# Two of seven output products moved into the last chunk slots of each scan, and two weight sums made by DMAs

## The chip, the cores and the metric

The kernel runs on one core of one Trainium2 chip. The metric is the device time of one execution in microseconds (us), taken as the median of several runs. TensorE (PE) does the matmuls, VectorE (DVE) and ScalarE (ACT) the elementwise work, GpSimd (POOL) some elementwise work and the issue of some DMAs, and SyncE (SP) issues the other DMAs.

## The reference

The program is a trunk of two layers over 1024 tokens of width 1024, all in float32. Cut to what matters here:

```
x = x + gated_deltanet(rmsnorm(x, norm_w[0]))      # layer 0: chunked delta rule, 16 heads of 128
x = x + mamba2(rmsnorm(x, norm_w[1]))              # layer 1: chunked state-space scan, 32 heads of 64
return rmsnorm(x, final_norm_w)
# the last line of both mixers is the one that the change is about
return o.reshape(b, t, 2048) @ w_out               # (1024 x 2048) @ (2048 x 1024)
```

## The kernel before

Each layer has three stages: input projections with causal convolutions, a scan over eight groups of heads (g = 0 to 7) with eight chunks each, and the output product `y @ w_out`. The work of a scan group is cut into eight slots; in each slot the program advances a few generators by one step: the scan itself (S), the preparation of the next group (I, J) and, in layer 1, `steps1`. A scheduler then sets the final order of the instructions of each engine, except where `keep_in_program_order` holds a DMA in place.

**The output product.** Its 2048 x 1024 weight is seen as a 2 x 2 block matrix, the tokens as two halves, and the product is done by a scheme with seven block products instead of eight. Each needs one weight form of `wf` (x00, s1, s2, x01, s3, s4, x11: a block or a sum of blocks) and one y form (`y_form`: a block of the scan's output or a sum of blocks). A block product has eight K tiles j and four token blocks p. Each of the 32 pairs takes three matmuls of 128 x 512 (`mac`, L411 to L413), because both operands are split into a high and a low part (`split`, L86 by ACT and L87 by DVE). So a product is 96 matmuls, 12 for each j, into four banks of PSUM: either `U` (names ps_proj, ps_pt) or `V` (ps_tr, ps_sc).

**Where the operands come from.** The scan writes its y rows to DRAM (`y0d`, L867 and L868 in layer 0; `y1d`, L1101 and L1103 in layer 1), and `load_y` (L359) reads them back in tiles of 128 x 512 through SP's queue. `load_x` (L383) does so for the weights. The sums of weight blocks differ by layer. In layer 1 they are ready in DRAM: `steps1` has made all four during the scan with 44 DMAs from POOL's queue, of which 16 copy (L338) and 28 accumulate (L340). In layer 0 nothing is made ahead: `w_form` loads the blocks of a sum and POOL adds them (L389). Products 1 and 2 keep the sum s1, s2 in SBUF (`W1`), product 4 (s3) loads two blocks for each j and adds them, product 5 (s4) adds x01 to W1. The y forms of products 1 and 2 go through `N1` (L371) and `Tt` (L374).

**Order of the products.** Product 0 (`early`) runs inside the last four slots of group 7, spread between the last chunk steps of the scan. Its result stays in its four PSUM banks. Then the memory pool of the scan is closed and another opened (`nrm`, tiles woh, wol, yh, yl, Tt, xrow, u). `rest` runs products 1 to 6: product 1 on the V banks, whose split tiles still lie in the old pool (name wy), while the new pool comes up. At product 1's j = 2 the residual rows start to be fetched (`fetch`, L445, twelve DMAs then and four later), ACT copies product 0's banks to `u` (L475), and DVE adds the banks to xrow (L454). Each later product is added to or subtracted from xrow directly (L454, L456) or through `u` (L460 on POOL, L463 on DVE); then comes the RMSNorm of finished rows.

**Names in the rows below.** L803, L811, L820, L838 and L840 are the matmuls of a chunk step of layer 0's scan, whose state S is carried from step to step; L66 transposes a finished head (yn); L867 gates it into the tile yg, and L868 stores that. In layer 1 L1072 to L1076 are the scan's last matmuls.

Of the kernel before, what the change touches and what calls it, by code (L numbers as in the profile page):

```python
# [8 lines left out]
F32 = mybir.dt.float32  # L9
F32R = mybir.dt.float32r  # L10
AF = mybir.ActivationFunctionType
ALU = mybir.AluOpType
# [4 lines left out]
P = 128  # L17
# [7 lines left out]
def hybrid_trunk(  # L25
# [6 lines left out]
    nc = tc.nc  # L32
    x, out = x[0], out[0]
# [284 lines left out]
                                fill=-1e30, base=0, channel_multiplier=-1)  # L318
        return t

    def weight_sums(w_out, nm):

        X = lambda c, k: w_out[k * 1024:(k + 1) * 1024, c * 512:(c + 1) * 512]
        parts = {"s1": ((1, 0), (1, 1)), "s2": ((1, 0), (1, 1), (0, 0)), "s3": ((0, 0), (1, 0)),
                 "s4": ((0, 1), (1, 0), (1, 1), (0, 0))}
        forms = {f"x{c}{k}": X(c, k) for c in range(2) for k in range(2)}
        for f in parts:
            forms[f] = tc.dram_tile([1024, 512], F32, name=f"wo_{nm}{f}")

        def steps():  # L330
            for q in range(4):
                r = slice(q * 256, (q + 1) * 256)
                for i in range(4):
                    for f, p in parts.items():
                        if i < len(p):
                            src, dst = X(*p[i])[r, :], forms[f][r, :]
                            if i == 0:
                                d = nc.gpsimd.dma_start(dst, src)  # L338
                            else:
                                d = nc.gpsimd.dma_start(dst, src, accum_op=ALU.add)  # L340
                            tc.keep_in_program_order(d)
                            yield

        return forms, steps()

    def out_proj(yd, X, made, resid):
# [8 lines left out]
        N1, W1 = [], []  # L355
# [6 lines left out]
        def y_form(i, j, Tt):  # L362
            if i in (0, 3, 5):
                return load_y(*{0: (0, 0), 3: (1, 0), 5: (1, 1)}[i], j)
            if i == 4:
                a, b = load_y(1, 1, j), load_y(0, 1, j, "raw")
                (nc.gpsimd if made else nc.vector).tensor_tensor(out=a, in0=a, in1=b, op=ALU.subtract)
                return a
            if i == 1:
                a, b, d = load_y(0, 0, j), load_y(0, 1, j, "raw"), N1[j // 4][:, j % 4, :]  # L370
                (nc.gpsimd if made else nc.vector).tensor_tensor(out=d, in0=a, in1=b, op=ALU.subtract)  # L371
            else:
                a, d = load_y(*{2: (1, 1), 6: (1, 0)}[i], j), Tt[:, j, :]
# [6 lines left out]
        def load_x(f, j):  # L380
            raw = wring.tile([P, 512], F32, tag=("wr", "wh", "wl")[ring_at[0] % 3], name="wr", bufs=3)
            ring_at[0] += 1
            nc.sync.dma_start(raw, X[f][j * P:(j + 1) * P, :])  # L383
            return raw

        def w_form(f, j):
            if made or f[0] == "x":
                return load_x(f, j)
            add = lambda d, a, b: nc.gpsimd.tensor_tensor(out=d, in0=a, in1=b, op=ALU.add)  # L389
            if f == "s3":  # L390
                a, b = load_x("x00", j), load_x("x10", j)
                add(a, a, b)
                return a
            d = W1[j // 4][:, j % 4, :]
            if f == "s1":
                add(d, load_x("x10", j), load_x("x11", j))
            else:
                add(d, d, load_x({"s2": "x00", "s4": "x01"}[f], j))
            return d

        def pieces(i, j, ring, Tt):
# [25 lines left out]

        banks0 = []

        def early():  # L430
            banks0.extend(U())
            yield from product(0, banks0, in_a(("a0", "a1", "a2", "a3")))

        def rest(npool, nw, on_rows, before_last=lambda: None):
            rows = {t: [npool.tile([P, D], F32, tag="xr", name="xrow", bufs=NT) for _ in range(4)] for t in range(2)}
            Tt = npool.tile([P, 8, 512], F32, tag="T", name="Tt", bufs=1)
            u = npool.tile([P, 4, 512], F32, tag="u", name="u", bufs=1)
            N1.extend(apool.tile([P, 4, 512], F32, tag="a0", name="N1", bufs=2) for _ in range(2))
            if not made:
                W1.extend(apool.tile([P, 4, 512], F32, tag="a1", name="W1", bufs=2) for _ in range(2))  # L440
            half = lambda t, p, c: rows[t][p][:, c * 512:(c + 1) * 512]

            def fetch(t, c):
# [11 lines left out]
                else:  # L455
                    nc.vector.tensor_tensor(out=v, in0=v, in1=pt, op=ALU.subtract)  # L456

            def put_u(t, p, c, op):
                v = half(t, p, c)
                nc.gpsimd.tensor_tensor(out=v, in0=v, in1=u[:, p, :], op=op)  # L460

            def grow(p, pt):
                nc.vector.tensor_tensor(out=u[:, p, :], in0=pt, in1=u[:, p, :], op=ALU.add)  # L463
# [6 lines left out]
            def first(t, p, c):  # L470
                sums[t, p] = rms_first(npool.tile([P, 512], F32, tag="sq", name="sq", bufs=1), rows[t][p], c)

            def d0():
                for p in range(4):
                    nc.scalar.copy(u[:, p, :], banks0[p])  # L475
                    put(0, p, 0, banks0[p], ALU.add)

            def d1(p, pt):
                put(1, p, 0, pt, ALU.add)
                put(1, p, 1, pt, ALU.subtract)  # L480

            def d2(p, pt):
                grow(p, pt)
# [13 lines left out]
                put(1, p, 0, pt, ALU.add)  # L497
                finish(1, p, 0)

            for i, done in ((1, d1), (2, d2), (3, d3), (4, d4), (5, d5)):  # L500
                banks = V() if i % 2 else U()
                for j, _ in enumerate(product(i, banks, in_a(("a2", "a3")) if i == 1 else ring, Tt)):
                    if (i, j) == (1, 2):
                        fetch(0, 0)
                        d0()
                    if (i, j) == (1, 4):
                        fetch(1, 0)
                        fetch(1, 1)
                    if (i, j) == (3, 3):
                        fetch(0, 1)  # L510
                if i == 5:
                    before_last()
                for p in range(4):
                    done(p, banks[p])
# [57 lines left out]
        return yd[g // 4, n // 4][(g % 4) * 256:(g % 4 + 1) * 256, (n % 4) * P:(n % 4 + 1) * P]  # L572

    yd0, yd1 = y_dram("y0d"), y_dram("y1d")
    wo1, steps1 = weight_sums(sw_out, "s")
    wo0 = {f"x{c}{k}": gw_out[k * 1024:(k + 1) * 1024, c * 512:(c + 1) * 512] for c in range(2) for k in range(2)}
    early0, rest0 = out_proj(yd0, wo0, False, lambda n: x[n * P:(n + 1) * P, :])
    early1, rest1 = out_proj(yd1, wo1, True, lambda n: x1d[n])

    with tc.tile_pool(name="gw", bufs=2) as gw:  # L580
# [360 lines left out]
        for g in range(8):  # L941
            J = todo["K"] if g == 0 else js_of(g)
            I = inverse(g + 1) if g < 7 else iter(())
            S = scan(g)
            for slot in range(8):
                if g == 7 and slot > 3:
                    next(early0)
                    if slot < 6:
                        next(early0)
                for c in "SIJ":  # L950
                    if c == "S":
                        next(S, None)
                    elif c == "I":
                        next(I, None)
                    else:
                        next(J, None)
            for _ in I:
                pass
            flush()
            next(S, None)  # L960
            if g < 6:
                for _ in k_products(g + 2):
                    pass
            elif g == 7:
                next(early0)
            next(S, None)
            if g < 7:
                z_weights(g + 1)
# [14 lines left out]
    with tc.tile_pool(name="bpool", bufs=2) as bpool, tc.tile_pool(name="sw", bufs=2) as sw:  # L983
# [145 lines left out]
        for g in range(-1, 8):  # L1129
            its = [bc_halves(g + 1) if g >= 0 else bc0, x_halves(g + 1)] if g < 7 else []  # L1130
            J = (y_ for it in its for y_ in it)
            S = scan(g) if g >= 0 else iter(())
            for slot in range(8):
                if g >= 0:
                    next(steps1, None)
                if g == 7 and slot > 3:
                    next(early1)
                    if slot < 6:
                        next(early1)
                next(S, None)  # L1140
                next(J, None)
            flush()
            if g == 7:
                next(early1)
            next(S, None)
            for _ in early1 if g == 7 else ():
                pass
            if g < 7:
                GS[g + 1]["zw"] = load_zw(bpool, sw_in, (g + 1) * 256, ("a2", "a3"), 2)
# [34 lines left out]
```

## Time and profile before

| what | us |
|---|---|
| median of 3 runs (range) | 2002.54 (1997.89 to 2002.66) |
| the profiled execution, its own time | 1990.88 |
| its span | 1989.1 |
| PE busy in the span | 1886.8 (95%) |
| DVE, ACT, POOL busy | 1427.4, 1078.9, 572.7 |
| scan groups of layer 0, PE busy share in 200 to 800 | 96.6% |
| scan groups of layer 1, PE busy share in 1200 to 1800 | 99.0% |

The profiled execution is 11.7 us (0.6%) shorter than the median of the runs, and outside its span lie 1.8 us. The rows in the section on the trace come from that execution, with times from the start of its span. Matmuls overlap in the pipeline, so a busy PE isn't always a PE at its full rate; the granted clock (PEclk) beside it says how fast TensorE was allowed to run, where 1.00 is 2.4 GHz.

### The profile page before, as it was taken

Reading aid. Unit: us, or ns where it says so; the run is one execution under the profiler, and the core shown is the slowest. Engines: PE = TensorE matmul, PEld = TensorE weight load, DVE = VectorE, ACT = ScalarE, POOL = GpSimd, SP = SyncE. Lnnn points to the kernel's source line nnn. Section 1 sums busy time; section 2 is a strip of 40 time slices with the busy share of each in tenths; the row PEclk is TensorE's granted clock in tenths of the full one; section 3 lists DMA queues with packets and bytes.
Section 4 is the critical chain, followed back from the end, with each engine's and each line's share of the span. In section 5 each row is a group of like instructions: output and inputs, shape, how many; then the busy total and the mean of one; then the engine's idle time right before and its main releaser. Section 6 shows DMA issues by size and latency. Waiting matters only on the chain.

```text
span 1989.1 us, 36021 instructions
## 1 busy us (share of the span) xinstructions
PE 1886.8 (95%) x12782; PEld 1611.4 (81%) x12782; DVE 1427.4 (72%) x3027; ACT 1078.9 (54%) x2933; POOL 572.7 (29%) x934
## 2 busy tenths in 40 slices
PE   7997999999999999998989999999999999999997
PEld 5776888888888888886777788888888888888786
DVE  5787786777668786847689777666576666757677
ACT  5635656565655756554435465454545555554453
POOL 1102111212122212104164033434343342434053
PEclk9997999999999999999999999999999999999999
DMA  4421322233142424237475245455464543246664
GB/s 141 117 54 46 88 67 76 75 71 83 43 104 49 104 49 106 71 106 243 149 262 170 75 146 120 117 130 119 115 135 116 117 99 82 80 127 195 228 225 148
DMA packets 252470, 231.10 MB, mean 116 GB/s; under 512 B 66897, under 2 KB 182274, under 8 KB 252290
## 3 DMA queue, kind: packets, MB, share of 16 engines
q1 hardware_dynamic: 242370, 205.73, 35.5%
q0 software_dynamic: 9920, 23.07, 6.2%
q8 instruction: 100, 1.64, 0.3%
q14 instruction: 80, 0.66, 0.1%
HBM read 199.19 MB, written 52.63 MB: 127 GB/s over the span
## 4 chain that ended last, share of the span: by engine, by line
PE 34%; DMA 6%; DVE 6%; POOL 2%; issue 2%; ACT 2%; SPq 0%; POOLq 0%; DVEq 0%; ACTq 0%
PE ps_proj L165 5%; PE ps_proj L166 4%; PE ps_proj L167 4%; DMA gcrow<-gcr_s 2%; PE ps_proj L227 2%; PE ps_proj L228 2%; PE ps_proj L229 2%; PE ps_sc L1075 1%; PE ps_tr L66 1%; DVE acc L204 1%; PE ps_proj L412 1%; DMA yr<-y0d 1%; PE ps_proj L413 1%; PE ps_pt L411 1%; PE ps_proj L411 1%
## 5 line engine op out<-in xcount | busy, mean ns | idle before, releaser
L165 PE MATMUL ps_proj<-hid_h,wh 128*128 128x512 f32 x1024 | 413.4, 404 | 4.9 <-ACT acc L200 3.2
L167 PE MATMUL ps_proj<-hid_h,wl 128*128 128x512 f32 x1024 | 404.4, 395 | 0.0
L166 PE MATMUL ps_proj<-hid_l,wh 128*128 128x512 f32 x1024 | 403.4, 394 | 0.0
L227 PE MATMUL ps_proj<-zh,hid_h 128*128 128x256 f32 x1024 | 300.1, 293 | 2.7 <-DVE z L234 2.7
L229 PE MATMUL ps_proj<-zh,hid_l 128*128 128x256 f32 x1024 | 296.1, 289 | 0.0
L228 PE MATMUL ps_proj<-zl,hid_h 128*128 128x256 f32 x1024 | 295.1, 288 | 0.0
L165 PEld LDWEIGHTS ps_proj<-hid_h,wh 128*128 128x128 f32 x1024 | 192.7, 188 | 45.9 <-ACT acc L200 4.1
L167 PEld LDWEIGHTS ps_proj<-hid_h,wl 128*128 128x128 f32 x1024 | 192.6, 188 | 40.8
L166 PEld LDWEIGHTS ps_proj<-hid_l,wh 128*128 128x128 f32 x1024 | 193.0, 189 | 35.9 <-issue 0.2
L227 PEld LDWEIGHTS ps_proj<-zh,hid_h 128*128 128x128 f32 x1024 | 196.7, 192 | 7.6 <-DVE z L234 4.0
L228 PEld LDWEIGHTS ps_proj<-zl,hid_h 128*128 128x128 f32 x1024 | 196.6, 192 | 3.0
L229 PEld LDWEIGHTS ps_proj<-zh,hid_l 128*128 128x128 f32 x1024 | 196.6, 192 | 0.3
L204 DVE SCALAR_TENSOR_TENSOR acc<-raw,cw_ssd,acc 128x512 f32<-128x512 f32 x192 | 160.2, 835 | 42.5 <-ACT acc L202 39.8
L204 DVE SCALAR_TENSOR_TENSOR acc<-raw,cw_gdn,acc 128x512 f32<-128x512 f32 x192 | 145.5, 759 | 17.4 <-ACT acc L200 15.9
L317 POOL TENSOR_SCALAR_AFFINE_SELECT gcrow<-gcrow 128x512 f32<-128x512 f32 x128 | 93.5, 734 | 189.1 <-DMA gcrow<-gcr_g 133.3
L853 POOL TENSOR_SCALAR so<-so,cq 128x2 f32<-128x2 f32 x64 | 28.2, 441 | 406.6 <-ACT yn L852 406.6
L87 DVE TENSOR_TENSOR wl<-wr,wh 128x512 fp32r<-128x512 f32 x128 | 89.6, 701 | 68.2 <-ACT wh L86 66.1
L184 ACT ACTIVATE th<-acc 128x512 f32<-128x512 f32 x128 | 80.1, 627 | 86.7 <-DVE acc L204 86.7
L662 DVE TENSOR_TENSOR tm<-Dt,X 128x2 f32<-128x2 f32 (+30 forms) x248 | 86.4, 348 | 46.7 <-POOL X L651 38.9
L86 ACT CAST wh<-wr 128x512 fp32r<-128x512 f32 x128 | 78.7, 616 | 69.9 <-PE ps_proj L166 60.6
L197 ACT COPY raw<-ps_proj 128x512 f32<-128x512 f32 x128 | 74.4, 581 | 75.4 <-PE ps_proj L167 71.2
L1046 ACT ACTIVATE lt<-gcrow,ldt_s 128x128 f32<-128x128 f32 x256 | 82.0, 391 | 41.6 <-DVE mt L1048 18.9
(316 smaller groups left out, 4474.3 us busy)
## 6 DMA issues: line engine op xcount, KB each, us to landing
wr<-in_gdn_w_in_dram SPq DMA_DIRECT2D x96, 256.0 KB, 3.0
wr<-in_ssd_w_in_dram SPq DMA_DIRECT2D x96, 256.0 KB, 2.9
wo_ss<-in_ssd_w_out_dram POOLq DMA_DIRECT2D x44, 512.0 KB, 6.6
wr<-in_gdn_w_out_dram SPq DMA_DIRECT2D x72, 256.0 KB, 4.2
yr<-y0d SPq DMA_DIRECT2D x72, 256.0 KB, 4.1
yr<-y1d SPq DMA_DIRECT2D x72, 256.0 KB, 3.7
gcrow<-gcr_g SPq DMA_DIRECT2D x64, 256.0 KB, 3.5
gcrow<-gcr_s SPq DMA_DIRECT2D x64, 256.0 KB, 4.0
```

What stands on the lines that cost most here:

```text
L87: nc.vector.tensor_tensor(out=lo, in0=src, in1=hi.bitcast(F32), op=ALU.subtract)
L165: nc.tensor.matmul(pt[0:nco], hi[:, j, 0:nco], xh[:, j, :], start=first, stop=False)
L166: nc.tensor.matmul(pt[0:nco], hi[:, j, 0:nco], xl[:, j, :], start=False, stop=False)
L167: nc.tensor.matmul(pt[0:nco], lo[:, j, 0:nco], xh[:, j, :], start=False, stop=last)
L184: nc.scalar.activation(th, src, AF.Tanh, scale=0.5)
L204: nc.vector.scalar_tensor_tensor(out=acc, in0=raw[:, k:k + 512], scalar=cw[:, k * 32 + ti:k * 32 + ti + 1], in1=acc, op0=ALU.mult, op1=ALU ...
L227: nc.tensor.matmul(pt, xh, zh[:, k, :], start=k == 0, stop=False)
L228: nc.tensor.matmul(pt, xh, zl[:, k, :], start=False, stop=False)
L229: nc.tensor.matmul(pt, xl, zh[:, k, :], start=False, stop=k == KT - 1)
L317: nc.gpsimd.affine_select(out=t, in_=t, pattern=[[0, 4], [1, P]], compare_op=ALU.is_ge, fill=-1e30, base=0, channel_multiplier=-1)
L662: nc.vector.tensor_tensor(out=tv, in0=Dt[:, r0:, s:], in1=X[:, s:s + 1, s:].to_broadcast([P, nr, nj]), op=ALU.mult)
L1046: nc.scalar.activation(lt[:, h, :], rows[h][:, n % 4, :], AF.Exp, bias=ldt[:, h0 + h, n:n + 1])
```

## The change

`early` now runs products 0 and 1, both inside slots 4 to 7 of group 7 (three steps in each slot, two more behind them, and what is left at the end). Both use the U banks, and ACT copies each result to SBUF tiles `M[0]` and `M[1]` (pool a, tag a0). The tiles N1 and W1 move to the tags a1 and a3, so the split tiles of both products share what is left of the old pool: two buffers in layer 0, four in layer 1. `rest` begins with product 2. The four copies L475 and the twelve adds from PSUM by which products 0 and 1 went into xrow are replaced by twelve adds from SBUF (`d01`: eight on POOL, four on DVE), and all twelve fetches are issued at product 2's j = 1.

In layer 0 the sums s3 and s4 are now made in DRAM by 24 DMAs on POOL's queue (`steps0`, 512 KB each, 8 copies and 16 accumulations), one in each of slots 1 to 3 of every group. Products 4 and 5 load them as one tile for each j; the 24 POOL adds for them go, and product 4's y subtraction goes from DVE to POOL in layer 0 too.

```
-    def weight_sums(w_out, nm):
+    def weight_sums(w_out, nm, which):
...
+        parts = {f: parts[f] for f in which}
...
-                (nc.gpsimd if made else nc.vector).tensor_tensor(out=a, in0=a, in1=b, op=ALU.subtract)
+                nc.gpsimd.tensor_tensor(out=a, in0=a, in1=b, op=ALU.subtract)
...
-            if made or f[0] == "x":
+            if f in X:
                 return load_x(f, j)
             add = lambda d, a, b: nc.gpsimd.tensor_tensor(out=d, in0=a, in1=b, op=ALU.add)
-            if f == "s3":
-                a, b = load_x("x00", j), load_x("x10", j)
-                add(a, a, b)
-                return a
             d = W1[j // 4][:, j % 4, :]
...
-                add(d, d, load_x({"s2": "x00", "s4": "x01"}[f], j))
+                add(d, d, load_x("x00", j))
...
         def early():
-            banks0.extend(U())
-            yield from product(0, banks0, in_a(("a0", "a1", "a2", "a3")))
+            M.extend(apool.tile([P, 4, 512], F32, tag="a0", name="M", bufs=2) for _ in range(2))
+            N1.extend(apool.tile([P, 4, 512], F32, tag="a1", name="N1", bufs=2) for _ in range(2))
+            if not made:
+                W1.extend(apool.tile([P, 4, 512], F32, tag="a3", name="W1", bufs=2) for _ in range(2))
+            for i in range(2):
+                banks = U()
+                yield from product(i, banks, in_a(("a2", "a3") if made else ("a2",)))
+                for p in range(4):
+                    nc.scalar.copy(M[i][:, p, :], banks[p])
...
-            u = npool.tile([P, 4, 512], F32, tag="u", name="u", bufs=1)
...
+            u, m = M
...
-            def d0():
+            def d01():
                 for p in range(4):
-                    nc.scalar.copy(u[:, p, :], banks0[p])
-                    put(0, p, 0, banks0[p], ALU.add)
-
-            def d1(p, pt):
-                put(1, p, 0, pt, ALU.add)
-                put(1, p, 1, pt, ALU.subtract)
+                    put_u(0, p, 0, ALU.add)
+                for p in range(4):
+                    put_u(1, p, 1, ALU.subtract, m, nc.vector)
+                    put_u(1, p, 0, ALU.add, m)
...
-            for i, done in ((1, d1), (2, d2), (3, d3), (4, d4), (5, d5)):
+            for i, done in ((2, d2), (3, d3), (4, d4), (5, d5)):
...
-                    if (i, j) == (1, 2):
+                    if (i, j) == (2, 1):
                         fetch(0, 0)
-                        d0()
-                    if (i, j) == (1, 4):
+                        fetch(1, 1)
                         fetch(1, 0)
-                        fetch(1, 1)
+                    if (i, j) == (2, 4):
+                        d01()
...
+    wo0, steps0 = weight_sums(gw_out, "g", ("s3", "s4"))
+    wo1, steps1 = weight_sums(sw_out, "s", ("s1", "s2", "s3", "s4"))
...
+                if 0 < slot < 4:
+                    next(steps0, None)
                 if g == 7 and slot > 3:
                     next(early0)
-                    if slot < 6:
-                        next(early0)
+                    next(early0)
                 for c in "SIJ":
                     if c == "S":
                         next(S, None)
+                        if g == 7 and slot > 3:
+                            next(early0)
...
             elif g == 7:
                 next(early0)
+                next(early0)
```

The order of PE's instructions at the end of layer 0's scan, before the change. The first rows are the last two chunk steps; product 1 (on ps_sc and ps_tr, its split tiles named wy) follows:

```order
L803 MATMUL ps_sc<-S,kT 128x256
L781 MATMUL ps_tr<-qT,kT 128x128
L811 MATMUL ps_sc<-vpp,nte 128x128 x2
L838 MATMUL ps_sc<-S,qT 128x256
L840 MATMUL ps_sc<-p,att 128x128 x2
L838 MATMUL ps_sc<-S,qT 128x256
L840 MATMUL ps_sc<-p,att 128x128 x2
L411 MATMUL ps_sc<-wy 128x512
L412 MATMUL ps_sc<-wy 128x512
L413 MATMUL ps_sc<-wy 128x512
```

The same place after the change. The first row is the last of product 1, which is now on ps_proj and ps_pt; the chunk step behind it is the last but one:

```order
L410 MATMUL ps_pt<-wy 128x512 x2
L803 MATMUL ps_sc<-S,kT 128x256
L66 MATMUL ps_tr<-ident,yn 128x128
L781 MATMUL ps_tr<-qT,kT 128x128
L66 MATMUL ps_tr<-ident,yn 128x128
L811 MATMUL ps_sc<-vpp,nte 128x128 x2
L820 MATMUL ps_sc<-p,ktok 128x128 x2
L838 MATMUL ps_sc<-S,qT 128x256
L840 MATMUL ps_sc<-p,att 128x128 x2
```

All 96 matmuls of product 1 have moved ahead of these steps. PE's next rows are the last chunk step, the transposes of the last heads, and the first two matmuls of product 2, whose split tiles woh, wol and yh lie in the new pool:

```order
L803 MATMUL ps_sc<-S,kT 128x256
L811 MATMUL ps_sc<-vpp,nte 128x128 x2
L838 MATMUL ps_sc<-S,qT 128x256
L840 MATMUL ps_sc<-p,att 128x128 x2
L838 MATMUL ps_sc<-S,qT 128x256
L840 MATMUL ps_sc<-p,att 128x128 x2
L66 MATMUL ps_tr<-ident,yn 128x128 x6
L408 MATMUL ps_proj<-woh,yh 128x512
L409 MATMUL ps_proj<-wol,yh 128x512
```

No output matmul stands between the last chunk steps and product 2 any more.

DVE's order at the start of product 2 in layer 0, before the change. Tt, wol and yl are product 2's operands, wy<-N and wy<-W those of product 1, and xrow<-ps_proj and xrow<-ps_pt are the adds of product 0's banks:

```order
L374 SCALAR_TENSOR_TENSOR Tt<-N_11766,yr 128x512 x3
L87 TENSOR_TENSOR wy<-W_11769,wy 128x512
L87 TENSOR_TENSOR wy<-N_11767,wy 128x512
L454 TENSOR_TENSOR xrow<-ps_proj,xrow 128x512
L87 TENSOR_TENSOR wol<-W_11768,woh 128x512
L454 TENSOR_TENSOR xrow<-ps_proj,xrow 128x512
L87 TENSOR_TENSOR wol<-W_11768,woh 128x512 x2
L454 TENSOR_TENSOR xrow<-ps_pt,xrow 128x512
L87 TENSOR_TENSOR wol<-W_11768,woh 128x512
L454 TENSOR_TENSOR xrow<-ps_pt,xrow 128x512
L87 TENSOR_TENSOR wy<-W_11769,wy 128x512
L87 TENSOR_TENSOR wy<-N_11767,wy 128x512
```

And after the change, where the adds into xrow take M from SBUF:

```order
L375 SCALAR_TENSOR_TENSOR Tt<-N_11403,yr 128x512 x3
L87 TENSOR_TENSOR wol<-W_11405,woh 128x512 x4
L87 TENSOR_TENSOR yl<-Tt,yh 128x512 x3
L462 TENSOR_TENSOR xrow<-xrow,M 128x512 x3
L87 TENSOR_TENSOR wol<-W_11406,woh 128x512
L462 TENSOR_TENSOR xrow<-xrow,M 128x512
L87 TENSOR_TENSOR wol<-W_11406,woh 128x512
L375 SCALAR_TENSOR_TENSOR Tt<-N_11403,yr 128x512
```

The operands of product 1 are gone from this place, and four adds from SBUF stand between the operands of j = 0 to 2 and the Tt of j = 3.

## Rows read from the trace of the kernel before

**Rows 1.** The page's first part: busy time, share and instructions of each engine.

```profile
PE 1886.8 (95%) x12782; PEld 1611.4 (81%) x12782; DVE 1427.4 (72%) x3027; ACT 1078.9 (54%) x2933; POOL 572.7 (29%) x934
```

**Rows 2.** Busy time by stretch: length, engines, then granted clock, DMA share, GB/s.

```profile
200.00:800.00 600.00, 579.35 (x4641) 510.73 (x4639) 442.13 (x1208) 373.66 (x1140) 119.85 (x231) 0.99 0.30 76
918.42:938.73 20.31, 12.38 (x62) 10.03 (x61) 12.58 (x28) 9.79 (x35) 12.85 (x12) 0.83 0.91 325
938.73:947.25 8.52, 6.66 (x38) 5.33 (x38) 3.71 (x12) 5.36 (x22) 1.32 (x4) 1.00 0.05 15
960.00:970.00 10.00, 6.96 (x23) 5.00 (x22) 7.11 (x12) 9.32 (x18) 1.83 (x1) 0.83 0.83 271
1040.00:1050.00 10.00, 6.68 (x23) 5.03 (x22) 9.02 (x9) 4.44 (x8) 6.08 (x4) 0.83 0.92 299
1200.00:1800.00 600.00, 594.02 (x4124) 511.12 (x4123) 398.73 (x722) 310.63 (x820) 226.12 (x400) 1.00 0.48 115
1880.00:1960.00 80.00, 80.00 (x354) 66.25 (x353) 63.50 (x79) 37.33 (x74) 34.63 (x29) 1.00 0.66 210
```

**Rows 3.** Timeline of PE, end of layer 0's scan: start, us, work [idle before].

```profile
918.42 0.71 PE L811 MATMUL ps_sc<-vpp,nte 128*128 128x128 f32 x4
...
938.73 0.48 PE L803 MATMUL ps_sc<-S,kT 128*128 128x256 f32 x1
...
963.25 0.50 PE L411 MATMUL ps_tr<-wy 128*128 128x512 f32 x1 [2.93 <-ACT wy L86]
...
968.62 0.39 PE L411 MATMUL ps_proj<-woh,yh 128*128 128x512 f32 x1
...
999.06 0.39 PE L411 MATMUL ps_tr<-woh,yh 128*128 128x512 f32 x1
```

**Rows 4.** Timeline of ACT, the same stretch.

```profile
956.48 0.48 ACT L867 ACTIVATE yg<-ps_tr,gnw_half 128x256 f32<-128x256 f32 x1 [1.94 <-DMA y0d<-yg]
...
960.63 1.07 ACT L475 COPY u<-ps_proj 128x512 f32<-128x512 f32 x2 [1.69 <-DMA y0d<-yg]
...
963.07 2.21 ACT L86 CAST woh<-W 128x512 fp32r<-128x512 f32 x4
```

**Rows 5.** Timeline of SP's queue, the same stretch.

```profile
961.01 7.40 SPq L445 DMA_DIRECT2D xrow<-in_x_dram  x12
968.81 1.00 SPq L359 DMA_DIRECT2D yr<-y0d  x2
```

**Rows 6.** DMA issues, 950 to 975: count, KB each, median us to landing.

```profile
yr<-y0d SPq DMA_DIRECT2D x3, 256.0 KB, 5.3
```

**Rows 7.** Timelines of DVE and POOL, two engines at the same time.

```profile
1002.86 0.70 DVE L87 TENSOR_TENSOR yl<-yr,yh 128x512 fp32r<-128x512 f32 x1 [1.01 <-ACT yh L86]
1003.48 1.78 DVE L87 TENSOR_TENSOR wol<-wr,woh 128x512 fp32r<-128x512 f32 x1
...
1002.98 6.84 POOL L460 TENSOR_TENSOR xrow<-xrow,u 128x512 f32<-128x512 f32 x4
```

**Rows 8.** PE's waits, 1000 to 1060: us in total, times, longest.

```profile
PE ps_proj L412 <- DVE wol L87: 4.9, 3, 3.3
PE ps_tr L412 <- DVE wol L87: 1.4, 1, 1.4
```

**Rows 9.** Timelines of PE and ACT, end of layer 1's scan and the products behind it.

```profile
1838.84 0.47 PE L411 MATMUL ps_sc<-wy 128*128 128x512 f32 x1
...
1847.96 1.08 ACT L475 COPY u<-ps_proj 128x512 f32<-128x512 f32 x2 [1.95 <-DMA y1d<-yg]
...
1854.65 0.77 PE L411 MATMUL ps_proj<-woh,yh 128*128 128x512 f32 x1 [3.36 <-DMA xrow<-x1d]
...
1889.06 0.39 PE L411 MATMUL ps_tr<-woh,yh 128*128 128x512 f32 x1
...
1910.82 0.39 PE L411 MATMUL ps_proj<-woh,yh 128*128 128x512 f32 x1
```

**Rows 10.** Layer 1's accumulating DMAs (L340): ns of one issue min, median, max.

```profile
L340 POOL DMA_DIRECT2D wo_ss<-in_ssd_w_out_dram x28: 902/990/1250, 1196.3 to 1620.8; - x28
```

More of the change, by code (lines that the diff above doesn't have):

```diff
@@ L426, in in_a @@
             return ring
-        banks0 = []
+        M = []
         def early():
-            banks0.extend(U())
-            yield from product(0, banks0, in_a(("a0", "a1", "a2", "a3")))
+            M.extend(apool.tile([P, 4, 512], F32, tag="a0", name="M", bufs=2) for _ in range(2))
[7 more added lines that the diff above has]
+                    nc.scalar.copy(M[i][:, p, :], banks[p])
         def rest(npool, nw, on_rows, before_last=lambda: None):
@@ L436, in rest @@
             Tt = npool.tile([P, 8, 512], F32, tag="T", name="Tt", bufs=1)
-            u = npool.tile([P, 4, 512], F32, tag="u", name="u", bufs=1)
-            N1.extend(apool.tile([P, 4, 512], F32, tag="a0", name="N1", bufs=2) for _ in range(2))
-            if not made:
-                W1.extend(apool.tile([P, 4, 512], F32, tag="a1", name="W1", bufs=2) for _ in range(2))
+            u, m = M
             half = lambda t, p, c: rows[t][p][:, c * 512:(c + 1) * 512]
@@ L456, in put, with put_u @@
                     nc.vector.tensor_tensor(out=v, in0=v, in1=pt, op=ALU.subtract)
-            def put_u(t, p, c, op):
+            def put_u(t, p, c, op, of=u, eng=nc.gpsimd):
                 v = half(t, p, c)
-                nc.gpsimd.tensor_tensor(out=v, in0=v, in1=u[:, p, :], op=op)
+                eng.tensor_tensor(out=v, in0=v, in1=of[:, p, :], op=op)
             def grow(p, pt):
@@ L498, in d5 @@
                 finish(1, p, 0)
-            for i, done in ((1, d1), (2, d2), (3, d3), (4, d4), (5, d5)):
+            for i, done in ((2, d2), (3, d3), (4, d4), (5, d5)):
                 banks = V() if i % 2 else U()
-                for j, _ in enumerate(product(i, banks, in_a(("a2", "a3")) if i == 1 else ring, Tt)):
-                    if (i, j) == (1, 2):
+                for j, _ in enumerate(product(i, banks, ring, Tt)):
+                    if (i, j) == (2, 1):
                         fetch(0, 0)
-                        d0()
-                    if (i, j) == (1, 4):
+                        fetch(1, 1)
                         fetch(1, 0)
-                        fetch(1, 1)
+                    if (i, j) == (2, 4):
+                        d01()
                     if (i, j) == (3, 3):
@@ L574, in hybrid_trunk @@
     yd0, yd1 = y_dram("y0d"), y_dram("y1d")
-    wo1, steps1 = weight_sums(sw_out, "s")
-    wo0 = {f"x{c}{k}": gw_out[k * 1024:(k + 1) * 1024, c * 512:(c + 1) * 512] for c in range(2) for k in range(2)}
+    wo0, steps0 = weight_sums(gw_out, "g", ("s3", "s4"))
+    wo1, steps1 = weight_sums(sw_out, "s", ("s1", "s2", "s3", "s4"))
     early0, rest0 = out_proj(yd0, wo0, False, lambda n: x[n * P:(n + 1) * P, :])
@@ L1137, in hybrid_trunk @@
                     next(early1)
-                    if slot < 6:
-                        next(early1)
+                    next(early1)
                 next(S, None)
+                if g == 7 and slot > 3:
+                    next(early1)
                 next(J, None)
@@ L1143, in hybrid_trunk @@
             if g == 7:
+                next(early1)
                 next(early1)
```

## The prediction

> **What bounds the kernel now.** I read the page's first part, then the busy time by stretch, then PE's timeline and waits where a stretch isn't full, and last the queues behind those waits. TensorE is busy for 95% of the span [rows 1]: what the change can give or take is PE's idle time and its time at a low clock. Most of the program has little to give: PE is busy 579 of 600 us in layer 0's scan and 594 of 600 in layer 1's [rows 2]. Three places are left.
>
> First, the end of layer 0's scan. From 918.42, where product 0 is done, to 938.73 PE works 12.4 of 20.3 us at a granted clock of 0.83: the chunk steps are a chain, and no output matmul is left to stand between them. Then it works 6.7 of 8.5 us for the last two steps [rows 2, 3]. Product 1 follows, stops for 2.93 us at 963.25 behind ACT's copies of product 0, and runs slowly until product 2 begins at 968.62 [rows 3, 4]; the clock of 960 to 970 is 0.83 [rows 2]. Product 2 is done at 999.06.
>
> Second, products 4 and 5 of layer 0. PE waits four times for wol, 4.9 + 1.4 = 6.3 us [rows 8], in the stage where each j needs two weight loads and a POOL add, and the clock falls to 0.83 in 1040 to 1050 [rows 2]. Layer 1, with ready sums, has PE busy 80.00 of 80 us in 1880 to 1960 [rows 2].
>
> Third, the end of layer 1's scan: one wait of 3.36 us for the fetch at 1854.65 [rows 9].
>
> PE's matmuls are the same before and after, so I add up waits and clock.
>
> **Products 4 and 5.** The change makes them like layer 1's, where that stretch is full. I take away the 6.3 us, and for the low clock 0.17 of some 8 us that PE then worked, 1.4: **-7.7 us**. It would be -6.3 if the clock fell for another reason, and -2 if only the queue for loads mattered, since the DMA share there is 0.92 at 299 GB/s [rows 2] and one load of two goes away.
>
> **End of layer 0's scan.** Now 192 output matmuls stand between chunk steps 2 to 5. A product lasts 1910.82 - 1889.06 = 21.8 us [rows 9], a j 2.7. Product 1 comes ahead of step 6, so step 6 begins at 918.42 + 21.8 + the PE time of what is left of steps 3 to 5. That time is 12.38 x 0.83 = 10.3 us if each matmul keeps the time it holds PE today, about half of it if the product's matmuls fill its gaps; I take 6.7, which two whole steps hold at full clock [rows 2]. So step 6 begins at 946.9, against 938.73. ACT's copies of product 0 are hidden, those of product 1 may cost 0.7: 947.6.
>
> Steps 6 and 7 and the last transposes are now bare. The two steps take 8.5 us as they do today. Their last y store landed at 960.63 [rows 4], 13.4 us behind the steps' end at 947.25; 12 of product 1's matmuls stood in between (2.7), so I take 10.7. The last store lands at 947.6 + 8.5 + 10.7 = **966.8**. Cover is gone here: in before, product 1 ran through the stores' landings.
>
> Product 2 can't start sooner, because its pool and Tt wait for that landing. On ACT's queue the casts woh come first, 2.21 us for four [rows 4], then yh: PE restarts 3.1 us behind the landing. j = 0 to 2, whose y tiles are loaded ahead, take 8.2 us and some 1.7 more, as PE comes back from idle at a low clock (963.25 to 968.62 shows it). So they last until landing + 13. Behind the landing SP issues nw and twelve fetches, 7.40 us, and only then the y tile of j = 3, as it did before (961.01, 968.81) [rows 5]; it lands 5.3 us later [rows 6], at landing + 13.1, and Tt, yh and yl need 2.3 more. This is the stall that comes in the place of those removed: at least 2.4 us. It is longer if DVE is late. Of POOL's eight adds into xrow each takes 1.7 us, and beside them a DVE operation with two SBUF inputs takes 1.78 instead of 0.70 [rows 7]; a j needs three of these on DVE (Tt, wol, yl), 5.3 us against PE's 2.7, for as long as POOL is busy, 13.7 us. Two or three j fit in there, each 2.6 us late, less what wol is ahead: up to 8 us. I take 5. With 13.6 us for j = 3 to 7 product 2 ends at 966.8 + 13 + 5 + 13.6 = 998.4.
>
> Product 1's supply must now keep up with the scan. It has two split buffers, N1 from DVE and W1 from POOL, and all loads while DMA share is 0.91 [rows 2]. Nothing shows this directly; the bounds are 0 and 8 us (a share of the 7.9 us in which PE idled there today), and I take 2.5. Together 1000.9 against 999.06: **+2 us**, between -5 (restart without a longer stall, short steps) and +11 (long stall, late supply).
>
> **End of layer 1's scan.** 36 of product 1's matmuls (8.2 us) come ahead of the last chunk's scan rows, 60 behind. The scan's end moves from 1838.84 to about 1845.5, as its small waits there are covered by 1.5 us. The last landing was 9.1 us behind the scan's end [rows 9] and now has 16 more product matmuls ahead of its transposes (3.6): 1858.2. PE restarts at 1861.3, having lost 2 us to 3 behind product 1. The y tile of j = 3 lands 13.1 behind the landing here too, so j = 3 starts at 1873.6 or later instead of 1869.5: 4 us at least, up to 10. The end of product 2 is 1861.3 + 21.8 + 4 to 10, or 1887 to 1893, against 1889.06 [rows 9]. I take **+1.5**, between -2 and +6.
>
> **Layer 0's scan groups.** 24 DMAs on POOL's queue, 0.99 us of POOL for one that accumulates [rows 10], or some 22 us of POOL in a stretch where it is busy 120 of 600 us [rows 2]. Layer 1 takes 44 such DMAs with PE busy 99%. The scheduler also sets the scan's other instructions in another order; of such a shift the trace shows no price, so I bound it by the waits there: PE idles 20.7 us in 600, and I allow a sixth of it either way. I take **+0.5**, between -3 and +4.
>
> The Trainium skill ("SBUF — State Buffer", section "SBUF: two separate sides") says that a DMA issued by GpSimd has its descriptors written there and is starved while VectorE runs a two-port operation, and advises the other queues. That would put some of the 16 accumulations late and the adds behind them too. Layer 1's row, with issues of 902 to 1250 ns, doesn't show much of it [rows 10]; by the rule the scan would cost as in rival 2, by the row nothing.
>
> **Sum.** -7.7 + 2 + 1.5 + 0.5 = **-3.7 us** on the profiled execution's 1990.88. That execution is 11.7 below the median of the runs; from the median 2002.54 the same step gives **1999 us**. Under 0.3% (6 us), which is about what runs of this kernel can tell from no change.
>
> **Rivals.**
> 1. *The cover holds.* PE restarts at the landing and finds j = 3 ready: the fetches are off its way and the copies to M free the banks early. Then layer 0 gives -5, layer 1 -2, products 4 and 5 -7.7: -14.7, 1988 us; half of the stalls gone gives -9, 1993 us. For it: today the chain's idle time is plain to see at 918 to 938, and 192 matmuls are there to fill it. Against: SP's order puts twelve fetches ahead of j = 3.
> 2. *Slower: POOL as the new bound in the scan.* The 24 DMAs stand in the queue ahead of POOL's small operations for the gated norm, and a chunk step waits for these. If each of 16 accumulations makes a step late by its 0.99 us, +16, by half of that +8; with the other terms +4 to +12, or 2010 us in the middle. It decides as soon as more than ten steps are late. Against it: layer 1's scan, with more of them, is full.
> 3. *Slower: DVE and POOL share what they need at the start of product 2.* With both stalls at their upper end and product 1's supply late, layer 0 +11, layer 1 +6, products 4 and 5 -7.7, scan +0.5: +10, 2012 us. It decides once the stalls come to 14 us in all. For it: 1.78 against 0.70 in one stage already [rows 7]. The Trainium skill says the same of the pair ("SBUF — State Buffer", section "Who interferes with whom"): a VectorE instruction with two SBUF inputs contends with a GpSimd instruction that reads SBUF, one with a single SBUF input doesn't; so by that rule the adds from PSUM that go were free of it, and the adds from M that come aren't. Rows 7 agree on the first half.
> 4. *The sums in DRAM don't help*: products 4 and 5 wait as before because the loads are the limit. Then only -2 comes from there: +2, 2004.5 us. This lies within no change.
>
> **How the numbers follow.** Forecast with rival 4: 0.39. Rival 1: 0.37. Rival 3: 0.13. Rival 2: 0.11. So faster by over 0.3% 0.37, within 0.39, slower 0.24. The range for 8 in 10 goes from rival 1's full gain, 1988, to rivals 2 and 3, 2011; the forecast's own is 1996.5 to 2008.5.
>
> **What would show it.** Right: in the products 4 and 5 of layer 0 no wait for wol over 0.5 us and clock 1.00; PE nearly full until step 6 and idle from there to a restart about 967 to 970; a wait of 2 to 8 us inside product 2 at j = 3, behind the yr load or behind DVE; PE busy near 579 of 600 in 200 to 800. Wrong: product 2 without a wait at j = 3 (rival 1), PE busy below 570 in 200 to 800 with waits that lead to POOL (rival 2), DVE's Tt, wol and yl at 1.78 through most of product 2 (rival 3).

## The result, and the profile after

The changed kernel takes 2023.06 us in the median of four runs (2018.32 to 2027.31), the kernel before 2000.31 in four. The ratio is 1.0113 with a 95% interval of 1.0079 to 1.0147: the change makes the kernel **slower by 22.6 us** (16 to 29). The forecast was 1999 us, no change, with a range up to 2011.

Single executions of one kernel differ by up to 1% here, so the sizes below come from ratios, each with its interval, and the traces serve to say where time goes and what is waited for. One thousandth of the time is 2 us.

The page's first part for the kernel after, its profiled execution being 2019.22 us long [rows 1]:

```profile
span 2017.5 us, 36080 instructions
...
PE 1894.5 (94%) x12782; PEld 1619.5 (80%) x12782; DVE 1413.7 (70%) x3003; ACT 1085.4 (54%) x2941; POOL 599.9 (30%) x966
```

Busy time by stretch after the change: length, then PE, PEld, DVE, ACT and POOL, then granted clock, DMA share and GB/s. The stretches are layer 0's scan groups, products 4 and 5 and what lies around them, the start of product 2 in layer 0, and that in layer 1:

```profile
200.00:800.00 600.00, 566.48 (x4508) 497.82 (x4507) 427.85 (x1150) 357.09 (x1088) 122.22 (x231) 0.97 0.35 85
1055.00:1098.00 43.00, 43.00 (x191) 35.65 (x190) 34.33 (x43) 23.07 (x48) 22.61 (x21) 1.00 0.69 215
990.00:1000.00 10.00, 2.33 (x6) 1.47 (x7) 4.81 (x10) 4.69 (x9) 1.22 (x3) 0.58 0.29 90
1000.00:1010.00 10.00, 10.00 (x35) 7.93 (x33) 8.29 (x9) 1.24 (x2) 8.16 (x6) 0.74 1.02 380
1010.00:1020.00 10.00, 4.04 (x11) 2.94 (x10) 10.00 (x12) 3.09 (x5) 5.05 (x4) 0.77 0.29 83
1900.00:1910.00 10.00, 8.21 (x27) 6.61 (x28) 6.08 (x9) 2.79 (x5) 0.53 (x1) 0.69 0.46 142
```

The second row is what the change was to give: PE is busy for all of 43 us at full clock, where before it waited 6.3 us and had a clock of 0.83 in one stretch [rows 2, 8]. From the first matmul of product 3 to the last output matmul of layer 0 it took 102.0 us (999.1 to 1101.1) and takes 92.1 (1032.8 to 1124.9). The other rows are what it cost. In the scan groups PE is busy 566 of 600 us, not 579, and the clock falls with it (0.97, from 0.99). The idle time grew by 12.9 us there; the lower clock, over some 570 us of work, is an estimated 11 more, though both clocks are rounded to 0.01. At the start of product 2 in layer 0 PE is nearly idle for 10 us, works at a clock of 0.74, and then stops again; layer 1 has the second of these stops alone.

**The scan groups.** PE's largest waits from 170 to 900 us, of before and then of after (us in total, times, longest). S is the scan's state, which DVE updates at the end of a chunk step:

```profile
PE ps_sc L803 <- DVE S L826: 5.1, 4, 2.4
```

```profile
PE ps_sc L803 <- DVE S L826: 16.6, 6, 6.1
```

What DVE was doing at one of these is seen around 475 to 494 us, in group 3, on four engines of the kernel after. `xd` is a place in DRAM through which the next group's blocks are rearranged (written by four DMAs, L647, and read back as X, L650), L651 a small POOL operation on X, L662 the first of DVE's steps of the inverse, L341 one of the 24 new DMAs:

```profile
475.05 0.88 POOL L341 DMA_DIRECT2D wo_gs<-in_gdn_w_out_dram  x1 [6.64 <-DMA wo_gs<-in_gdn_w_out_dram]
```

```profile
475.98 4.49 SPq L647 DMA_DIRECT2D xd<-nte  x4
...
484.89 1.13 SPq L650 DMA_DIRECT2D X<-xd  x2
```

```profile
489.71 0.16 POOL L651 MEMSET X<- 128x32 f32 x1 [9.00 <-DMA gcrow<-gcr_g]
```

```profile
489.91 0.16 DVE L662 TENSOR_TENSOR tm<-Dt,X 128x2 f32<-128x2 f32 x1 [5.63 <-POOL X L651]
...
492.89 0.34 DVE L826 SCALAR_TENSOR_TENSOR S<-S,egl_g,ps_sc 128x128 f32<-128x128 f32 x1
```

```profile
493.64 1.22 PE L803 MATMUL ps_sc<-S,kT 128*128 128x256 f32 x2 [5.14 <-DVE S L826]
```

Read from the bottom: PE waits 5.14 us for S; S stands in DVE's queue behind the first steps of the inverse; these wait 5.63 us for POOL; and POOL waits for loads on SP's queue. The loads are late because the writes of xd are: four issues take 4.49 us, and X can be loaded 8.9 us after the first of them. The same place before the change:

```profile
460.39 2.24 SPq L647 DMA_DIRECT2D xd<-nte  x4
466.33 1.13 SPq L650 DMA_DIRECT2D X<-xd  x2
```

There it took 5.9 us. A write of xd landed 3.7 us after its issue in the median, and 5.2 after the change; the slowest took 4.7 and 8.6. Rows of DMA landing (us min/median/max) for L647, before and after:

```profile
DMA to landing us min/median/max: 2.3/3.7/4.7
```

```profile
DMA to landing us min/median/max: 2.3/5.2/8.6
```

Added up over the eight trips, the time from the first write of xd to the first load of X is 42.1 us before and 58.4 after. Layer 0's scan has a second trip through DRAM, `dd`, written at L668 and read back at L673 later in the group: its eight come to 32.6 us before and 32.8 after, so it isn't slower.

**Product 2.** Timelines of PE, DVE and POOL at its start in layer 0, after the change:

```profile
999.02 0.76 PE L408 MATMUL ps_proj<-woh,yh 128*128 128x512 f32 x1 [6.54 <-ACT yh L86]
1016.30 0.80 PE L408 MATMUL ps_proj<-woh,yh 128*128 128x512 f32 x1 [5.96 <-ACT yh L86]
```

```profile
1004.26 4.62 DVE L462 TENSOR_TENSOR xrow<-xrow,M 128x512 f32<-128x512 f32 x3 [1.71 <-DMA xrow<-in_x_dram]
1008.81 1.78 DVE L87 TENSOR_TENSOR wol<-W,woh 128x512 fp32r<-128x512 f32 x1
1010.51 1.75 DVE L462 TENSOR_TENSOR xrow<-xrow,M 128x512 f32<-128x512 f32 x1
1012.18 1.75 DVE L87 TENSOR_TENSOR wol<-W,woh 128x512 fp32r<-128x512 f32 x1
1013.85 2.35 DVE L375 SCALAR_TENSOR_TENSOR Tt<-N,yr 128x512 f32<-128x512 f32 x2
1016.12 0.68 DVE L87 TENSOR_TENSOR wol<-W,woh 128x512 fp32r<-128x512 f32 x1
```

```profile
1001.84 11.54 POOL L462 TENSOR_TENSOR xrow<-xrow,M 128x512 f32<-128x512 f32 x7 [10.54 <-DMA xrow<-in_x_dram]
```

POOL's row shows the first seven of its eight adds. Beside them DVE's operations take 1.5 to 1.8 us each, and the Tt of j = 3 comes behind 9.6 us of them, at 1013.85; once the adds are done, wol takes 0.68 (the last of DVE's rows). Product 2 lasts 33.9 us, of which 21.8 are matmuls at full clock. Layer 1 has the same wait at j = 3, and PE's first 96 matmuls from the start of product 2 last 32.6 us (a few of product 3's come in before the last of product 2):

```profile
1901.79 0.80 PE L408 MATMUL ps_proj<-woh,yh 128*128 128x512 f32 x1 [7.58 <-ACT yh L86]
```

### The profile page after: what moved, and what is told of

Its sections match the earlier page's. It is cut to its first block, busy times and chain, and to the rows that moved or that the text cites. A ratio compares the mean times of both kernels' runs of the same rounds, so it can differ in the third digit from the quotient of the medians.

```text
span 2017.5 us, 36080 instructions
## 1 busy us (share of the span) xinstructions
PE 1894.5 (94%) x12782; PEld 1619.5 (80%) x12782; DVE 1413.7 (70%) x3003; ACT 1085.4 (54%) x2941; POOL 599.9 (30%) x966
## 4 chain that ended last, share of the span: by engine, by line
PE 63%; DMA 11%; DVE 10%; ACT 4%; issue 3%; POOL 3%; SPq 1%; POOLq 0%; DVEq 0%; ACTq 0%
PE ps_proj L165 8%; PE ps_proj L166 8%; PE ps_proj L167 7%; PE ps_proj L227 4%; PE ps_proj L229 4%; PE ps_proj L228 4%; PE ps_tr L66 2%; DVE acc L204 2%; DMA gcrow<-gcr_s 2%; DMA gcrow<-gcr_g 1%; PE ps_proj L408 1%; PE ps_pt L66 1%; PE ps_sc L1079 1%; PE ps_proj L409 1%; DMA X<-xd 1%
## 5 line engine op out<-in xcount | busy, mean ns | idle before, releaser
L165 PEld LDWEIGHTS ps_proj<-hid_h,wh 128*128 128x128 f32 x1024 | 193.1, 189 | 40.2 <-ACT gtmp L268 0.8
L662 DVE TENSOR_TENSOR tm<-Dt,X 128x2 f32<-128x2 f32 (+30 forms) x248 | 86.3, 348 | 53.3 <-POOL X L651 46.2
```

Of the source, the lines that this page charges most:

```text
L165: nc.tensor.matmul(pt[0:nco], hi[:, j, 0:nco], xh[:, j, :], start=first, stop=False)
L662: nc.vector.tensor_tensor(out=tv, in0=Dt[:, r0:, s:], in1=X[:, s:s + 1, s:].to_broadcast([P, nr, nj]), op=ALU.mult)
```

## The experiments

The theories after the result: A, the 24 DMAs in slots 1 to 3 slow layer 0's scan; B, product 1 in its last slots slows it; C, the fetches and the adds of M hold up product 2. Twelve kernels were run; each ratio is to the kernel before on the same chip. Kernels 1 to 4, 5 to 8, 9 and 10, and 11 and 12 each shared a chip, so some differences below, such as 10 against 4, are taken between ratios of two chips.

| kernel | ratio | interval |
|---|---|---|
| the change | 1.0113 | 1.0079 to 1.0147 |
| 1 no DMAs | 1.0058 | 1.0038 to 1.0078 |
| 2 small DMAs | 1.0048 | 1.0024 to 1.0073 |
| 3 DMAs alone | 1.0082 | 1.0055 to 1.0109 |
| 4 late slots | 1.0041 | 1.0021 to 1.0060 |
| 5 copies | 1.0071 | 1.0049 to 1.0092 |
| 6 DMAs alone, late slots | 0.9969 | 0.9951 to 0.9987 |
| 7 as 6, and layer 1's products | 1.0010 | 0.9992 to 1.0029 |
| 8 late slots, late fetch | 0.9996 | 0.9980 to 1.0012 |
| 9 DMAs alone, groups 1 to 6 | 0.9975 | 0.9954 to 0.9995 |
| 10 late slots, no adds of M | 0.9978 | 0.9965 to 0.9991 |
| 11 full DMAs to no use | 1.0201 | 1.0163 to 1.0238 |
| 12 the same in two parts | 1.0186 | 1.0148 to 1.0223 |

**1. No DMAs.**

```
-    wo0, steps0 = weight_sums(gw_out, "g", ("s3", "s4"))
+    wo0, steps0 = weight_sums(gw_out, "g", ())        # w_form adds s3, s4 on POOL as before
```

> The change without the 24 DMAs of layer 0: products 4 and 5 add their weight blocks on POOL as before, all else is the change. PE's order in layer 0's scan is then that of before. Theory A (the DMAs cost the scan its 22 us): the scan is back at before's time, what stays is the slower stage of products 0 to 2 in layer 0 (about +12) and layer 1's (+5), and products 4 and 5 gain nothing: about 2017 us. Rival B (the scan is slower because product 1 was put into its last slots): the 22 us stay and the 10 us of products 4 and 5 are lost too: about 2033 us.

Measured +11.6 us. The scan is back (PE busy 580.61 of 600 us in 200 to 800), so B falls; products 0 to 2 of both layers cost what is left, less than the 17 that theory A expected. The change costs 11.0 us more than this kernel; with the 9.9 that products 4 and 5 give, the scan pays some 21 (13 to 29).

**2. Small DMAs.**

```
+                            if only:
+                                src, dst = src[0:16, :], dst[0:16, :]
```

> As the run without the DMAs, but with 24 DMAs in the same slots that move 16 rows each (32 KB) to a place in DRAM that nobody reads, instead of 256 rows (512 KB). Theory A1 (what costs is the bytes, which hold up the other DMAs of the scan): as without the DMAs within 3 us, about 2018. Rival A2 (what costs is their issue on POOL's queue, 0.99 us each, ahead of POOL's small operations): 10 to 20 us above the run without DMAs, about 2030.

Measured +9.6 us, no more than without DMAs: A1. 24 issues on POOL's queue cost nothing that can be measured.

**3. DMAs alone.**

```
+    wo0, steps0 = weight_sums(gw_out, "g", ("s3", "s4"))      # in the kernel before
...
+                if 0 < slot < 4:
+                    next(steps0, None)
```

> The kernel before with the 24 DMAs alone: products 4 and 5 of layer 0 load ready sums, products 0 and 1 stay where they were. Theory A: the scan costs about +22, products 4 and 5 give 10 back: about 2012 us. Rival B: the scan is as before and only the gain is seen: about 1990 us.

Measured +16.4 us. With the 9.9 that products 4 and 5 give, the scan pays some 26 (21 to 32) here.

**4. Late slots.**

```
-                if 0 < slot < 4:
+                if slot > 3 and g < 6:
```

> The change with the 24 DMAs in slots 4 to 7 of groups 0 to 5 instead of slots 1 to 3 of all eight. Theory A3 (the DMAs cost what they do because they run beside the writes of xd and the loads of X and gcrow, which the next group's inverse waits for): these get their old time back, 10 to 20 us less than the change, 2003 to 2013 us. Rival A4 (any place in the scan is as bad): as the change, about 2023 us.

Measured +8.2 us, 14 less than the change: A3. In the group shown above xd is written and X loaded in 3.6 us, by this kernel's queue of SP:

```profile
476.55 1.95 SPq L647 DMA_DIRECT2D xd<-nte  x4
...
480.10 1.13 SPq L650 DMA_DIRECT2D X<-xd  x2
```

PE is busy 580 of 600 us in its scan with the same bytes moved. POOL's accumulating DMAs wait for one another as long as in the change (19.9 us, against 15.6), so such waits by themselves are harmless there.

One trip of this kernel does meet two of the DMAs, in group 0. On SP's queue, POOL and PE:

```profile
158.32 2.12 SPq L647 DMA_DIRECT2D xd<-nte  x4
169.38 1.13 SPq L650 DMA_DIRECT2D X<-xd  x2
```

```profile
158.82 1.03 POOL L341 DMA_DIRECT2D wo_gs<-in_gdn_w_out_dram  x1 [0.26 <-issue]
...
159.54 1.27 POOL L341 DMA_DIRECT2D wo_gs<-in_gdn_w_out_dram  x1
...
174.14 0.16 POOL L651 MEMSET X<- 128x32 f32 x1 [6.45 <-DMA X<-xd]
```

```profile
177.34 1.22 PE L803 MATMUL ps_sc<-S,kT 128*128 128x256 f32 x2 [6.31 <-DVE S L823]
```

It takes 11.1 us, where this kernel's other seven take 3.5 to 6.2, and PE's longest wait between 170 and 900 us follows. No load of gcrow stands between: POOL waits for X itself.

**5. Copies.**

```
-                                d = nc.gpsimd.dma_start(dst, src, accum_op=ALU.add)
+                                d = nc.gpsimd.dma_start(dst, src)        # layer 0 alone
```

> The change with its 16 accumulating DMAs of layer 0 as plain copies, so that the sums s3 and s4 lack their later blocks; the order of every engine is that of the change. In the change an accumulating DMA lands 7.1 us after its issue, a copy after 4.8. Theory D1 (the traffic costs the scan its time): the xd round trip gets shorter and 5 to 12 us of the change's 22.6 come back, 1.006 to 1.009 of before. Rival D2 (the scan's other order costs it, the DMAs only happen to be there): as the change, 1.011.

Measured +14.2 us, 8 less than the change (0 to 16), with every engine's order the same: D1. In the group shown above:

```profile
473.27 2.73 SPq L648 DMA_DIRECT2D xd<-nte  x4
...
478.53 1.14 SPq L651 DMA_DIRECT2D X<-xd  x2
```

That is 5.3 us, but others of its groups stay at 7 to 7.9. Most of the cost remains, so this alone doesn't rule the order out. Two things fell together, too: these 16 DMAs land after 4.5 us instead of 6.8 (the 7.1 and 4.8 of the expectation mix both layers), and POOL waits 8.9 us for earlier ones instead of 15.6. Kernel 12 tells these apart.

**6. DMAs alone, in late slots.** The kernel of 3 with the edit of 4.

> The kernel before with the 24 DMAs alone, in slots 4 to 7 of groups 0 to 5. Theory A3: the scan costs at most 3 us and products 4 and 5 give 8 to 10: 5 to 10 us faster than before, 0.995 to 0.9975. Rival A4 (the place doesn't matter): as with the DMAs in slots 1 to 3, 1.008.

Measured -6.2 us (-10 to -3): A3, and a version that beats both kernels.

**7. Layer 1's products as well.** Kernel 6 with layer 1's output product and slots from the change (`out_proj1` is the change's `out_proj`).

```
-    early1, rest1 = out_proj(yd1, wo1, True, lambda n: x1d[n])
+    early1, rest1 = out_proj1(yd1, wo1, True, lambda n: x1d[n])
```

> As the kernel before with the 24 DMAs in the late slots, and the change's products 0 and 1 in layer 1 alone. By the traces of before and the change layer 1 lost 5.4 us up to the end of product 2, so 4 to 6 us more than with the late DMAs alone (+0.002 to +0.003). If layer 1's loss came from layer 0's side (another state of queues and clock), no difference.

Measured 8.2 us more than kernel 6. So products 0 and 1 in layer 1's last slots cost some 8 us, and those in layer 0's, by the difference of 4 and 7, some 6.

**8. Late fetch.**

```
-                    if (i, j) == (2, 1):
+                    if (i, j) == (2, 5):
...
-                    if (i, j) == (2, 4):
+                    if (i, j) == (2, 7):
                         d01()
```

> The change with the 24 DMAs in the late slots, the twelve fetches at product 2's j = 5 instead of j = 1, and the adds from M at j = 7 instead of j = 4. Theory C (product 2 waits because fetches stand ahead of the y tile of j = 3 and the adds beside its operands): product 2 takes about 22 to 24 us instead of 33 in each layer, 12 to 18 us less than with the late DMAs alone, 0.995 to 0.998 of before. Rival C2 (the wait moves to product 3, whose operands then stand beside the adds): within 5 us of the late DMAs alone, 1.002 to 1.004.

Measured 9 us less than kernel 4, between C and C2. Product 2 lasts 27.4 us in layer 0 and 27.2 in layer 1, where C expected 22 to 24, with shorter waits, now for wol. PE's timeline in this kernel, layer 0 and layer 1:

```profile
1004.47 0.50 PE L409 MATMUL ps_proj<-wol,yh 128*128 128x512 f32 x1 [2.83 <-DVE wol L87]
...
1885.24 0.50 PE L409 MATMUL ps_proj<-wol,yh 128*128 128x512 f32 x1 [2.65 <-DVE wol L87]
```

**9. DMAs alone, groups 1 to 6.**

```
-                if slot > 3 and g < 6:
+                if slot > 3 and 0 < g < 7:
```

> The kernel before with the 24 DMAs alone, in slots 4 to 7 of groups 1 to 6 (with groups 0 to 5 the xd round trip at 157 us took 11.4 us instead of 6.6). PE's order in layer 0's scan is that of before to the last instruction. Theory A3: the scan costs 0 to 3 us, products 4 and 5 give 8 to 10: 0.995 to 0.997 of before, and every xd round trip within 2 us of before's. Rival (DMAs in any slots cost the scan through POOL or the DMA engines): no better than with groups 0 to 5, 0.997 to 1.000.

Measured -5 us, just inside the rival's range, with an interval that covers both: not told apart. The trips of xd are back at 4.2 to 6.8 us, the one in group 0 at 5.9 instead of kernel 6's 11.4, but the kernel is no faster than 6.

**10. No adds.**

```
-                    if (i, j) == (2, 4):
-                        d01()
```

> The change with the 24 DMAs in the late slots and without the twelve adds of M into xrow in each layer, so the output lacks products 0 and 1 there; the fetches stay where the change has them, and PE's and SP's order is that of the kernel with the adds. Theory C3 (the wait inside product 2 comes from the adds, which hold DVE): product 2 takes 24 us or less instead of 33 in each layer, 12 to 18 us less than with them, 0.995 to 0.998 of before. Theory C4 (it comes from the y tile of j = 3, whose load stands behind twelve fetches): a wait of 4 to 6 us in each layer stays, and 4 to 8 us come back, 1.000 to 1.002.

Measured 12.6 us less than kernel 4: C3. What C4 named is there too, but small. PE's timeline at j = 3 of product 2, layer 0 and layer 1:

```profile
1000.88 0.50 PE L408 MATMUL ps_proj<-woh,yh 128*128 128x512 f32 x1 [0.79 <-ACT yh L86]
...
1880.48 0.50 PE L408 MATMUL ps_proj<-woh,yh 128*128 128x512 f32 x1 [3.10 <-ACT yh L86]
```

Product 2 lasts 25.9 us, and layer 1's first 96 matmuls from there 26.0, a little more than the 24 of C3. Layer 0's restart wait (6.55 us) stays, since no matmul covers the last stores.

**11 and 12. The order or the bytes.** With the longer DMAs the scheduler also sets the scan in another order: the traces of kernels 2 and 11 differ from PE's 1648th matmul on, at 271 us. These two kernels tell that from the traffic. Kernel 11 is kernel 2 with `src[0:256, :]`; kernel 12 issues these bytes in two DMAs:

```
+                            for h in range(2 if only else 1):
+                                s_, d_ = (src[h * 128:(h + 1) * 128, :], dst[h * 128:(h + 1) * 128, :]) if only else (src, dst)
```

> As the run with 24 small DMAs (products 4 and 5 of layer 0 add on POOL, the DMAs write a place that nobody reads), but with the change's 256 rows (512 KB) each in slots 1 to 3; the order of PE in the scan is then the change's. Both theories expect 16 to 26 us more than with small DMAs: 1.013 to 1.018 of before.

> As the run with full DMAs, the same bytes in the same slots, but each DMA in two of 128 rows. The scheduler then leaves PE's order in the scan almost as before (256 lines differ from the kernel with small DMAs, 1558 from the one with full ones). Theory E1 (the bytes cost the scan its time, whatever the order): within 5 us of full DMAs, 1.011 or more. Rival E2 (the other order, which the scheduler made for the long DMAs, costs it): within 5 us of small DMAs, 1.003 to 1.007.

Measured +40.2 and +37.2 us, more than either theory expected of kernel 11, and E1. With nearly the old order and the same bytes the scan loses as much; with the old order and few bytes (kernel 2) nothing. Nor is it POOL's waits for earlier accumulations: these are 6.7 us in kernel 12 and 15.7 in 11. PE's wait for S in 170 to 900 us, of small DMAs, of the two parts, and of full DMAs:

```profile
PE ps_sc L809 <- DVE S L832: 5.7, 3, 3.4
```

```profile
PE ps_sc L809 <- DVE S L832: 17.4, 5, 4.6
```

```profile
PE ps_sc L809 <- DVE S L832: 18.9, 8, 5.7
```

Full DMAs cost 31 us more than small ones (22 to 40); kernel 3 gave some 26 and the change against kernel 1 some 21, which is within the intervals.

The trips of xd go with the losses through all kernels. Added up over the eight groups, in the profiled executions, they take 42 us before and 40 to 43 in kernels 1, 2, 4 and 6 to 10, where the scan has no large DMAs or has them in the late slots; they take 50 in kernel 5, 54 in 12, 58 in the change, 60 in 11 and 62 in 3.

## Why the prediction was wrong

**The step that failed is "Layer 0's scan groups: +0.5, between -3 and +4".** Measured: some 26 us from kernel 3, 31 from kernels 2 and 11, 21 from the change against kernel 1. It priced the 24 DMAs by POOL's time to issue them and took layer 1's full scan [rows 2, 10] as cover. Kernel 2 shows that the issue was rightly put at nothing. What was left out is what the bytes meet: layer 0's scan has a round trip through DRAM for each group, on SP's queue, and its writes land later beside the new transfers. The DMA share of 0.30 over 600 us looked like room, but the trip and the new DMAs fall into the same slots. Layer 1 was no evidence, for it has no such trip. Rival 2 had the place right and the mechanism wrong: not POOL's small operations wait, but X, and through it DVE's queue, S, and PE; so also its price was too low. Its sign came all the same (PE busy below 570 of 600 us, with waits that lead to POOL), but POOL itself waits there for the loads. The Trainium skill ("DMA: Bandwidth & Descriptors", section "Queues, rings and completion order") says that each DMA engine takes turns between the queues that have work for it; the slower writes of xd, 5.2 us instead of 3.7, agree with it.

The rule of the Trainium skill that was weighed in that step ("SBUF — State Buffer", section "SBUF: two separate sides"), that two-port operations of VectorE starve a DMA issued by GpSimd, isn't needed: the 16 accumulating DMAs land after 6.8 us in layer 0's scan, as layer 1's did before the change, and what is late are SP's.

**End of layer 0's scan: +2, measured +6** (kernels 4 and 7). The chain was right: bare steps 6 and 7, last landing 16.9 us behind step 6's start (19.2 predicted), restart 2.8 us behind the landing (3.1). The 10.7 us in it rest on a misreading: 24 of product 1's matmuls, not 12, stand ahead of the last transposes in the kernel before (from 947.7 to 953.6). Product 2 lasted 33.9 us, where the sum had 28.5. The mis-sized term is what follows the wait at j = 3: j = 3 to 7 took 16.6 us, put at 13.6, because PE comes back from this second stop at a low clock (0.70 from 1016.3 to 1026.3), which the sum had only for the first. The wait itself took 5.96, put at 5, and j = 0 to 2 took 11.3, put at 9.9. Late supply of product 1, put at 2.5, shows in no wait of PE for wy.

**End of layer 1's scan: +1.5, measured some 8** (kernel 7 against 6). The interval of such a difference is about 5 us either way, so it may be the +6 that the bounds allowed. The wait of 7.58 us lies inside the 4 to 10; the clock of 0.69 behind it was left out.

**Rival 3 was right as a mechanism** in both layers, and the likeliest step had half of it. Taking the adds away (kernel 10) gives 12.6 us back; the y tile behind twelve fetches, to which the forecast gave the first 2.4 us, counts for 0.8 and 3.1.

**Products 4 and 5: -7.7, measured -9.9.** Right, with PE full and at full clock. The figure is of single executions, but the other traces agree: products 3 to 6 take 91.6 to 92.4 us in the nine kernels that load ready sums, and 102.0 to 105.3 in the five that add them.

By experiments the terms make 16.4 + 6.2 + 8.2 = 31 us, above the 22.6 of the change. Each has an interval of 4 to 5 us either way; whether the rest is chance, or the parts overlap, stays open; the change against kernel 1 would give the scan some 5 us less than kernel 3 does. Open too is how much of the scan's loss came through the trip of xd alone and how much through the loads of gcrow beside it; only the DMAs' place and bytes were varied. At 158 us in kernel 4 the trip alone was enough. And kernel 9 leaves open what the DMAs cost in the best slots.

## What to carry to other kernels

A DMA that is off every critical path still has a price where it runs beside a small transfer that is on one: look for round trips through DRAM in the same slots before reading a low mean DMA share as room. Evidence from another stage counts only if that stage has the same waits. And when work moves from PSUM to SBUF, count which engine pair then reads SBUF at once, and add the clock that PE loses after each new stop.

## What the hardware showed

Bytes, not issues: 24 DMAs of 32 KB cost nothing, 24 of 512 KB in the same slots about 31 us, and 48 of 256 KB the same within 3 us, whatever the order. The same 24 of 512 KB, moved to slots where all but one trip goes without them, cost some 4 us (kernel 6) to 7 (kernel 4 against 1), by the 9.9 that products 4 and 5 give. DVE operations with two SBUF inputs took 1.5 to 1.8 us instead of 0.68 beside POOL's adds in both layers, as [rows 7] had shown in one.
